# Three stacks of shifted copies, GpSimd's norm sums over six tiles, and the mean read from its PSUM bank in a convolution layer

## The chip, the cores and the metric

The kernel runs on one core of a Trainium2 chip. The metric is the device time of one execution in microseconds (us), the median of several runs. The program is a decoder trunk of two residual layers over 512 positions of 1024 channels, in float32, with nearly all of its products made of three passes over split high and low parts.

## The reference, cut to what matters

Only the second (odd) layer's mixer changes. It is a Conformer convolution module:

```python
def causal_dwconv(x, w, b):                      # depthwise: one filter of width 31 per channel
    y = lax.conv_general_dilated(x, w[:, None, :], (1,), [(k_width - 1, 0)], ..., feature_group_count=ch)
    return y + b

def layer_norm(x, g, b):                         # over the 1024 channels of each position
    mu = jnp.mean(x, axis=-1, keepdims=True)
    xc = x - mu
    return xc * lax.rsqrt(jnp.mean(xc * xc, axis=-1, keepdims=True) + EPS) * g + b

def conformer_conv(h, w_pw1, dw_w, dw_b, ln_g, ln_b, w_pw2):
    a, g = jnp.split(h @ w_pw1, 2, axis=-1)
    u = a * jax.nn.sigmoid(g)
    u = causal_dwconv(u, dw_w, dw_b)
    u = jax.nn.silu(layer_norm(u, ln_g, ln_b))
    return u @ w_pw2
```

## The kernel before

Channels lie on the 128 partitions, positions along the free axis, so that the layer's 1024 channels are eight tiles of 128x512. For each tile i of 0 to 7 the function `conv(i)` adds these tasks to a plan:

- two products with `w_pw1` (`gemm`: load the raw weights, high part on ScalarE, low part on VectorE, 24 matmuls each), scaled, put through the sigmoid and multiplied to `u` (`gated`);
- the 31 taps of the filter, shared out over the engines. The first `4*FOURS[i]` taps run on TensorE, four taps to a group: `spill` writes `u` to DRAM (`d`, two buffers), four `fetch` transfers bring it back shifted by 0 to 3 positions into a `stack` tile (four channel groups of 32, each with four shifted copies), and each task `four(m)` is four small matmuls of `stack` with diagonal weights `dg`. I call the run of these for tile i "the fours of tile i"; ahead of them two matmuls `mean(0)`, `mean(1)` (line 737) put the negative mean of the first tile into the bank as a pivot. The next `ON_G[i]` taps go through ScalarE (`tap_s`) and GpSimd (`tap_g`, line 771), and the rest through VectorE (`tap_v`, line 786) on a bank of their own where the tile is in `APART`;
- two additions (`total`, line 801) that join the parts: first `y2`, then the tile `v[:, i]`, and ScalarE's square of it (line 805).

LayerNorm needs the sum over all channels of `v` and of its square. For tiles below `ON_PE` = 4 GpSimd adds them into `sv` and `sq` (lines 821, 823); each of the tiles 4 to 7, and then `sv` and `sq`, is given to TensorE, which sums over partitions with the constant matrix `ones_m` (line 859) into two banks, `mu` and `m2`. The order there is tile 4, tile 5, the GpSimd sums, tile 6, tile 7, mean and square each.

The order of all this is not the loop's. `Plan.issue` is a small list scheduler that runs when the program is built: each task has an engine, a cost, a key (smaller goes first), tasks it follows, and slots (buffers) that it takes and gives back. It picks, among the tasks that could start within 0.15 of the earliest, the one with the smallest key, and so fixes the order of every engine's queue and of SyncE's transfers. `four` tasks have the key i - 2, the `w_pw1` products i + 0.4j - 6.2, and the sums 4.9 for the first three steps and 5.1 for the last two. There are two stacks: tile i uses `stack[i % 2]`, and its fetches wait for the fours of tile i - 2.

After the plan, VectorE reads the two banks through a 32x32 transposition (`fold`, line 177), works out the variance on 16 columns, spreads the mean again over a whole tile `mus` (`unfold`, line 181), and then goes through the eight tiles: subtract the mean (line 883), multiply by the reciprocal deviation (line 887), Silu twice on ScalarE (lines 888, 889), low part (line 892). The products with `w_pw2` (lines 934 to 938, then 159 to 161) follow. Their weights are loaded and split (lines 139, 144) outside the plan, at places that the tile framework chooses in the queues.

Of the kernel before, what the change touches and what calls it, by code (L numbers as in the profile page):

```python
# [10 lines left out]
F32 = mybir.dt.float32  # L11
F32R = mybir.dt.float32r
AF = mybir.ActivationFunctionType
ALU = mybir.AluOpType
AX = mybir.AxisListType

P = 128
T = 512
D = 1024
KT = D // P  # L20
# [7 lines left out]
CW = 31  # L28
# [68 lines left out]
def hybrid_trunk(ctx: ExitStack, tc: tile.TileContext, x, prm, w_qk, w_v, w_f, w_u, w_pool,  # L97
                 w_out, w_pw1, w_dw, w_pw2, w_up, w_down, out):
    nc = tc.nc
    V, S, G, PE = nc.vector, nc.scalar, nc.gpsimd, nc.tensor  # L100
# [79 lines left out]
    def unfold(dst, src):  # L180
        V.transpose(out=dst.rearrange("p (a b) -> p a b", b=32), in_=src.to_broadcast([P, TC, 32]))
# [7 lines left out]
    class Normed:  # L189
# [10 lines left out]
        def add(self, k):  # L200
            split(res["x"][:, k], self.h[:, k], self.l[:, k], col(self.g, self.goff + k))
            if k == 0:
                S.activation(out=self.s, in_=res["x"][:, k], func=AF.Square)
            else:
                sq = self.tmp.tile([P, T], F32, tag="tt", name="sq")
                S.activation(out=sq, in_=res["x"][:, k], func=AF.Square)
                V.tensor_tensor(out=self.s, in0=self.s, in1=sq, op=ALU.add)
# [400 lines left out]
    FOURS = (0, 2, 1, 5, 3, 4, 5, 5)  # L608
    ON_G = (14, 11, 10, 9, 8, 5, 3, 2)
    APART = (0, 1, 2, 4, 5, 6, 7)  # L610
    ON_PE = 4

    def odd_layer(nrm, next_norm):
        with tc.tile_pool(name="cnv", bufs=1) as cv, tc.tile_pool(name="cnv2", bufs=2) as c2, \
# [2 lines left out]
                tc.tile_pool(name="cnvd", bufs=2, space=bass.MemoryType.DRAM) as dr:  # L617
            v = cv.tile([P, KT, T], F32, name="v")
            ones_t = cv.tile([P, P], F32R, name="ones_t")
            w4 = cv.tile([P, KT * 32], F32, name="w4")  # L620
            nc.sync.dma_start(out=w4, in_=w_dw)
            eye = cv.tile([P, 2, 32], F32, name="eye")[:, 0:1]
            fourth = [slice(32 * q, 32 * q + 32) for q in range(4)]
            for q in fourth:
                V.tensor_copy(out=eye[q, 0], in_=ident[q, q])
            stack = [cv.tile([P, 4, CW + T], F32, name=f"stack{i}") for i in range(2)]
            for st in stack:
                G.memset(st[:, :, 0:CW], 0.0)
            sv = cv.tile([P, T], F32, name="sv")
            sq = cv.tile([P, T], F32, name="sqs")  # L630
            mus = cv.tile([P, T], F32, name="mus")
            rs = cv.tile([P, T], F32, name="rs")
            zh = cv.tile([P, KT, T], F32R, name="zh")

            dg = cv.tile([P, sum(FOURS), 4, 32], F32, tag="zl", name="dg")
            for i in range(KT):
                m0, m1 = sum(FOURS[:i]), sum(FOURS[:i + 1])
                if m0 < m1:
                    n = 4 * FOURS[i]
                    wi = w4[:, 32 * i:32 * i + n].rearrange("p (m o) -> p m o", o=1)  # L640
                    G.tensor_tensor(out=dg[:, m0:m1].rearrange("p m g c -> p (m g) c"),
                                    in0=eye.to_broadcast([P, n, 32]),
                                    in1=wi.to_broadcast([P, n, 32]), op=ALU.mult)
# [2 lines left out]
            V.tensor_copy(out=ones_t, in_=rs[:, 0:P])  # L646


            v0, v0h, v0l = mus, zh[:, KT - 2], zh[:, KT - 1]

            plan = Plan({"pe": 0.0, "v": -4.0, "s": -4.0, "g": -4.0, "sp": -12.0},
                        {"raw": 3, "wh": 3, "wl": 3, "ps": 3, "s": 4, "o": 1, "a": 2, "tt": 2,
                         "u": 4, "d": 2, "stack0": 1, "stack1": 1, "y2": 2, "tap": 6})
            add = plan.add
            r_known = add(None, 0.0, 0.0, None, lag=5.0)
            squares, gemms = {}, []
# [1 line left out]
            def conv(i, pivot, sums):  # L658
# [63 lines left out]
                u = add("v", 0.7, key, gated, t0, t1, z, lag=0.05, give=[tag0, "tt"])  # L722
# [4 lines left out]
                    nc.sync.dma_start(out=mine["d"], in_=mine["u"][:, CW - 3:])  # L727

                def fetch(n):
                    nc.sync.dma_start(out=stack[i % 2][fourth[n], :, CW:],  # L730
                                      in_=mine["d"][:, 3 - n:3 - n + T].rearrange(
                                          "(g c) t -> c g t", c=32))

                def mean(n):
                    if n == 0:
                        mine["c"] = bank("s")
                    PE.matmul(mine["c"], lhsT=ones_t, rhs=(v0h, v0l)[n], start=(n == 0), stop=False)

                def four(m):
                    for g in range(4):  # L740
                        PE.matmul(mine["c"][fourth[g]], lhsT=dg[:, sum(FOURS[:i]) + m, g],  # L741
                                  rhs=stack[i % 2][:, g, CW - 4 * m:CW - 4 * m + T],
                                  start=False, stop=(m == FOURS[i] - 1))

                used, parts = [], []
                if i > 0:
                    st = f"stack{i % 2}"
                    t = add("sp", 0.5, -9.0, spill, u, lag=2.2, take=["d"])
                    t = add(None, 0.0, 0.0, None, t, take=[st])
                    used = [add("sp", 0.45, -9.0, lambda n=n: fetch(n), t, lag=4.0)  # L750
                            for n in range(4)]
                    add(None, 0.0, 0.0, None, *used, give=["d"])
                    t = add("pe", 0.23, i - 2.0, lambda: mean(0), pivot[0], take=["s"])
                    t = add("pe", 0.23, i - 2.0, lambda: mean(1), pivot[1], t)
                    for m in range(FOURS[i]):
                        t = add("pe", 0.94, i - 2.0, lambda m=m: four(m), t, *used,
                                give=[st] * (m == FOURS[i] - 1))
                    parts.append(t)
# [11 lines left out]
                def tap_g(s):  # L770
                    G.tensor_tensor(out=mine["y2"], in0=mine["y2"], in1=mine[s], op=ALU.add)  # L771

                g = b = add("s", 0.8, i + 2.8, begin_g, u, take=["y2"])
                for s in range(s0 + 1, s1):
                    t = add("s", 0.71, i + 2.8, lambda s=s: tap_s(s), b, take=["tap"])
                    g = add("g", 1.5, i + 2.8, lambda s=s: tap_g(s), g, t, lag=0.1, give=["tap"])
# [23 lines left out]
                def total(out, acc, y2):  # L800
                    V.tensor_tensor(out=out, in0=mine[acc], in1=y2, op=ALU.add)
# [5 lines left out]
                if i > 0:  # L807
                    key = i + 2.4
                    if i in APART:
                        g = add("v", 0.7, key, lambda: total(mine["y2"], "e", mine["y2"]), g, t,  # L810
                                give=["s"])
# [5 lines left out]
                    q = add("s", 0.63, key, square, t, take=["a"])  # L817
                    if i >= ON_PE:
                        sums[2].append((t, q))
                    else:  # L820
                        sums[0] = add("g", 1.28, i + 5.0, lambda: G.tensor_tensor(
                            out=sv, in0=sv, in1=y, op=ALU.add), t, sums[0])
                        sums[1] = add("g", 1.28, i + 5.0, lambda: G.tensor_tensor(
                            out=sq, in0=sq, in1=squares[i], op=ALU.add), q, sums[1], give=["a"])
# [24 lines left out]
            pivot, sums = None, None  # L849
            for i in range(KT):  # L850
                pivot, sums = conv(i, pivot, sums)
# [4 lines left out]
            def summed(name, tag, what, first, last):  # L856
                if first:
                    ms[name] = bank(tag)
                PE.matmul(ms[name], lhsT=ones_m, rhs=what(), start=first, stop=last)  # L859

            steps = [(*sums[2][i - ON_PE], lambda i=i: v[:, i], lambda i=i: squares[i])
                     for i in range(ON_PE, KT)]
            steps.insert(2, (sums[0], sums[1], lambda: sv, lambda: sq))
            for n, (*done, a, b) in enumerate(steps):
                for j, (name, tag, what) in enumerate((("mu", "o", a), ("m2", "ps", b))):
                    first, last = n == 0, n == len(steps) - 1
                    ms[name, "t"] = add(
                        "pe", 0.87, 4.9 if n < 3 else 5.1,
                        lambda name=name, tag=tag, what=what, first=first, last=last: summed(
                            name, tag, what, first, last),  # L870
                        done[j], *((gemms[-1],) if first else (ms[name, "t"],)),
                        take=[tag] if first else [],
                        give=["a"] if j == 1 and done[j] is not sums[1] and not last else [])
# [5 lines left out]
            mu, m2 = ms["mu"], ms["m2"]  # L879
            zl = cv.tile([P, KT, T], F32R, tag="zl", name="zl")  # L880

            def less_mean(k):
                V.tensor_tensor(out=v[:, k], in0=v[:, k], in1=mus, op=ALU.subtract)

            def parts_of(k):
                y, g, b = v[:, k], col("ln_g", k), col("ln_b", k)
# [8 lines left out]
            with tc.manual_schedule(engines={ENGINES["v"]}):  # L895
                mu16 = fold(mu, c2)
                var = cv.tile([P, TC, 1], F32, name="var")
                V.tensor_tensor(out=var, in0=mu16, in1=mu16, op=ALU.mult)
                unfold(mus, mu16)
                m216 = fold(m2, c2)  # L900
                V.tensor_tensor(out=var, in0=m216, in1=var, op=ALU.subtract)
                V.tensor_scalar(out=var, in0=var, scalar1=0.0, scalar2=None, op0=ALU.max)
                less_mean(0)
                r16 = inv_sqrt(var, c2)
                unfold(rs, r16)
                parts_of(0)
                for k in range(1, KT):
                    less_mean(k)
                    parts_of(k)
                    if k > 1:  # L910
                        low_part(k - 2)
                low_part(KT - 2)
                low_part(KT - 1)
# [166 lines left out]
```

## Time and profile before

| what | value |
|---|---|
| time, median of 3 runs | 1114.05 us (1112.44 to 1114.14) |
| the profiled execution's own time | 1112.13 us |
| its span, first to last instruction | 1110.4 us |
| TensorE's matmuls busy | 1088.5 us, 98% of the span |
| VectorE busy | 739.0 us, 67% |
| ScalarE busy | 512.2 us, 46% |
| GpSimd busy | 141.0 us, 13% |
| granted TensorE clock, mean | 0.998 of full |

Busy times are sums of the instructions' own times. The convolution layer takes some 180 us of the span, from about 570 to about 750 us; GpSimd works almost only there. In the rows below, DVE is VectorE, ACT ScalarE, POOL GpSimd, PE TensorE, SPq the queue of SyncE that issues transfers, and L801 is line 801 of the kernel. "bank" is any PSUM bank. A float32 matmul is shown as two passes, so that the 20 matmuls of five fours stand as x40, and one sum of line 859 as x2.

### The profile page before, as it was taken

The numbers are of one execution on the slowest core, as the hardware profiler recorded it, in microseconds if no ns is written. First come the engines' busy times: TensorE is split into PE (matmuls) and PEld (weight loads), VectorE is DVE, ScalarE is ACT, GpSimd is POOL, SyncE is SP. The second block draws the span as 40 slices with busy tenths as digits, with TensorE's granted clock in tenths as the row PEclk, the third lists the DMA queues.
The fourth block names the chain that finished last, engine by engine and source line by source line (L and its number), as shares of the span: only waits on it lengthen the run. The fifth ranks groups of instructions, "written<-read, shape, count | busy, mean of one in ns | idle before, by whom it ended". The sixth has DMA issues, their size and how long they took to land.

```text
span 1110.4 us, 12890 instructions
## 1 busy us (share of the span) xinstructions
PE 1088.5 (98%) x4950; PEld 878.9 (79%) x4950; DVE 739.0 (67%) x1046; ACT 512.2 (46%) x717; POOL 141.0 (13%) x124
## 2 busy tenths in 40 slices
PE   9999989999999999999999998999999999999998
PEld 7777777888888888888878763788888888888886
DVE  6888986677777777433359997777777777762221
ACT  6666754444444444322238563654444444431220
POOL 0133340000000000000038994000000000000000
PEclk9999999999999999999999999999999999999999
DMA  6311025233333322333235647032233323224340
GB/s 216 104 56 39 25 79 171 95 95 95 98 101 102 97 96 90 86 104 103 93 100 147 172 110 189 9 126 94 97 100 103 99 95 95 95 86 123 105 124 19
DMA packets 37406, 111.97 MB, mean 101 GB/s; under 512 B 4192, under 2 KB 4832, under 8 KB 37344
## 3 DMA queue, kind: packets, MB, share of 16 engines
q1 hardware_dynamic: 37344, 111.14, 32.7%
q8 instruction: 39, 0.64, 0.2%
q14 instruction: 23, 0.19, 0.1%
HBM read 107.18 MB, written 3.94 MB: 100 GB/s over the span
## 4 chain that ended last, share of the span: by engine, by line
PE 88%; DVE 6%; ACT 2%; DMA 1%; issue 1%; POOL 1%; SPq 0%; ACTq 0%; POOLq 0%; DVEq 0%
PE bank L160 28%; PE bank L161 28%; PE bank L159 28%; PE bank L741 1%; POOL us L422 1%; PE bank L859 1%; DMA stack<-d 1%; DVE wl L144 1%; PE bank L934 1%; PE bank L935 0%; DMA raw<-in_w_qk 0%; ACT wh L139 0%; PE bank L540 0%; DVE fold L177 0%; PE bank L938 0%
## 5 line engine op out<-in xcount | busy, mean ns | idle before, releaser
L159 PE MATMUL bank<-xh,wh 128*128 128x512 f32 x936 | 369.1, 395 | 1.3 <-ACT wh L257 1.3
L160 PE MATMUL bank<-xl,wh 128*128 128x512 f32 x936 | 365.5, 391 | 0.0
L161 PE MATMUL bank<-xh,wl 128*128 128x512 f32 x936 | 365.4, 390 | 0.0
L139 ACT ACTIVATE wh<-raw 128x1024 fp32r<-128x1024 f32 (+2 forms) x186 | 190.2, 1025 | 266.7 <-PE bank L160 229.3
L144 DVE TENSOR_TENSOR wl<-raw,wh 128x1024 fp32r<-128x1024 f32 (+1 forms) x176 | 213.9, 1217 | 141.3 <-ACT wh L139 139.4
L159 PEld LDWEIGHTS bank<-xh,wh 128*128 128x128 f32 x936 | 176.2, 188 | 41.4 <-issue 2.3
L161 PEld LDWEIGHTS bank<-xh,wl 128*128 128x128 f32 x936 | 176.0, 188 | 37.3 <-issue 0.7
L160 PEld LDWEIGHTS bank<-xl,wh 128*128 128x128 f32 x936 | 176.2, 188 | 37.0 <-issue 1.4
L159 PE MATMUL bank<-ah,wh 128*128 128x512 f32 x352 | 136.9, 389 | 0.0
L160 PE MATMUL bank<-al,wh 128*128 128x512 f32 x352 | 136.9, 389 | 0.0
L161 PE MATMUL bank<-ah,wl 128*128 128x512 f32 x352 | 136.9, 389 | 0.0
L971 DVE SCALAR_TENSOR_TENSOR y<-u,pt,y 128x511 f32<-128x511 f32 (+1 forms) x176 | 131.6, 748 | 7.8 <-ACT y L968 4.7
L966 DVE TENSOR_TENSOR u<-bank,rstd 128x512 f32<-128x512 f32 x88 | 60.5, 688 | 79.1 <-PE bank L161 79.1
L771 POOL TENSOR_TENSOR y<-y,tap 128x512 f32<-128x512 f32 x54 | 80.2, 1487 | 12.8 <-ACT tap L768 9.6
L166 ACT ACTIVATE ah<-y 128x512 fp32r<-128x512 f32 x44 | 27.8, 632 | 115.0 <-DVE y L976 115.0
L159 PEld LDWEIGHTS bank<-ah,wh 128*128 128x128 f32 x352 | 66.1, 188 | 13.8
L161 PEld LDWEIGHTS bank<-ah,wl 128*128 128x128 f32 x352 | 66.1, 188 | 13.7
L160 PEld LDWEIGHTS bank<-al,wh 128*128 128x128 f32 x352 | 66.1, 188 | 13.6
L968 ACT ACTIVATE y<-u,pt 128x512 f32<-128x512 f32 x88 | 71.3, 810 | 5.0 <-DVE u L966 3.9
L975 ACT ACTIVATE y<-y 128x512 f32<-128x512 f32 x44 | 27.8, 633 | 82.9 <-DVE y L971 82.8
L219 DVE TENSOR_TENSOR xr<-bank,xr 128x512 f32<-128x512 f32 x32 | 22.0, 690 | 60.5 <-PE bank L161 60.5
L786 DVE SCALAR_TENSOR_TENSOR bank<-u,pt,bank 128x512 f32<-128x512 f32 x79 | 56.4, 749 | 1.5 <-ACT bank L782 0.8
(197 smaller groups left out, 1061.3 us busy)
## 6 DMA issues: line engine op xcount, KB each, us to landing
raw<-in_w_up SPq DMA_DIRECT2D x88, 512.0 KB, 3.4
raw<-in_w_down SPq DMA_DIRECT2D x32, 512.0 KB, 3.5
raw<-in_w_pw SPq DMA_DIRECT2D x24, 512.0 KB, 3.8
stack<-d SPq DMA_DIRECT2D x28, 256.0 KB, 4.9
raw<-in_w_down SPq DMA_DIRECT2D x16, 384.0 KB, 3.2
xr<-in_x SPq DMA_DIRECT2D x16, 256.0 KB, 5.6
raw<-in_w_out SPq DMA_DIRECT2D x8, 512.0 KB, 3.4
raw<-in_w_qk SPq DMA_DIRECT2D x6, 512.0 KB, 3.5
```

Source lines behind the costliest of these rows:

```text
L139: S.activation(out=wh, in_=raw, func=AF.Copy)
L144: on.tensor_tensor(out=wl, in0=raw, in1=wh.bitcast(F32), op=ALU.subtract)
L159: PE.matmul(acc, lhsT=ah, rhs=bh, start=(first and i == 0), stop=False)
L160: PE.matmul(acc, lhsT=ah, rhs=bl, start=False, stop=False)
L161: PE.matmul(acc, lhsT=al, rhs=bh, start=False, stop=(last and i == n - 1))
L166: S.activation(out=h, in_=src, func=AF.Copy)
L771: G.tensor_tensor(out=mine["y2"], in0=mine["y2"], in1=mine[s], op=ALU.add)
L786: V.scalar_tensor_tensor(out=acc, in0=shifted(s), scalar=wcol(s), in1=acc, op0=ALU.mult, op1=ALU.add)
L966: V.tensor_tensor(out=u, in0=acc, in1=nrm.r, op=ALU.mult)
L968: S.activation(out=y, in_=u, func=AF.Identity, scale=col("cv_w", 3 * ct + 2), bias=col("cv_b", ct))
L971: V.scalar_tensor_tensor(out=y[:, s:], in0=u[:, 0:T - s], scalar=col("cv_w", 3 * ct + 2 - s), in1=y[:, s:], op0=ALU.mult, op1=ALU.add)
L975: S.activation(out=ys[0], in_=ys[0], func=AF.Silu)
```

## The change

- A third stack: tile i uses `stack[i % 3]`, so that its fetches wait for the fours of tile i - 3.
- `ON_PE` is 6: GpSimd adds the tiles 0 to 5, and TensorE sums only tile 6, the GpSimd sums, and tile 7, in this order. The first two of these steps have the key 4.9.
- VectorE subtracts the mean from `mu`, the PSUM bank itself; the tile `mus` and the `unfold` into it are gone.
- Memory: `dg`, `sv` and `w4` become parts of one tile `room` in the place that `zl` takes later, and the first tile's intermediate `v0` lies in `v[:, 7]` instead of `mus`.

```diff
-    ON_PE = 4
+    ON_PE = 6
...
-            w4 = cv.tile([P, KT * 32], F32, name="w4")
+            room = cv.tile([P, KT * T], F32, tag="zl", name="room")
+            DG = sum(FOURS) * P
+            dg = room[:, 0:DG].rearrange("p (m g c) -> p m g c", g=4, c=32)
+            sv = room[:, DG:DG + T]
+            w4 = room[:, DG + T:DG + T + KT * 32]
...
-            stack = [cv.tile([P, 4, CW + T], F32, name=f"stack{i}") for i in range(2)]
+            stack = [cv.tile([P, 4, CW + T], F32, name=f"stack{i}") for i in range(3)]
...
-            sv = cv.tile([P, T], F32, name="sv")
-            mus = cv.tile([P, T], F32, name="mus")
-            dg = cv.tile([P, sum(FOURS), 4, 32], F32, tag="zl", name="dg")
...
-            v0, v0h, v0l = mus, zh[:, KT - 2], zh[:, KT - 1]
+            v0, v0h, v0l = v[:, KT - 1], zh[:, KT - 2], zh[:, KT - 1]
...
-                         "u": 4, "d": 2, "stack0": 1, "stack1": 1, "y2": 2, "tap": 6})
+                         "u": 4, "d": 2, "stack0": 1, "stack1": 1, "stack2": 1, "y2": 2, "tap": 6})
...
-                    nc.sync.dma_start(out=stack[i % 2][fourth[n], :, CW:],
+                    nc.sync.dma_start(out=stack[i % 3][fourth[n], :, CW:],
...
-                                  rhs=stack[i % 2][:, g, CW - 4 * m:CW - 4 * m + T],
+                                  rhs=stack[i % 3][:, g, CW - 4 * m:CW - 4 * m + T],
...
-                    st = f"stack{i % 2}"
+                    st = f"stack{i % 3}"
...
-            steps.insert(2, (sums[0], sums[1], lambda: sv, lambda: sq))
+            steps.insert(-1, (sums[0], sums[1], lambda: sv, lambda: sq))
...
-                        "pe", 0.87, 4.9 if n < 3 else 5.1,
+                        "pe", 0.87, 4.9 if n < len(steps) - 1 else 5.1,
...
-                V.tensor_tensor(out=v[:, k], in0=v[:, k], in1=mus, op=ALU.subtract)
+                V.tensor_tensor(out=v[:, k], in0=v[:, k], in1=mu, op=ALU.subtract)
...
-                unfold(mus, mu16)
```

## Rows read from the trace of the kernel before

**Rows 1.** A window of 10 us: busy of PE, PEld, DVE, ACT, POOL; clock; DMA share, GB/s.

```profile
670.00:680.00 10.00, 6.88 (x50) 2.24 (x50) 9.46 (x15) 5.74 (x9) 9.48 (x8) 1.00 0.80 179
```

**Rows 2.** The chain that ended last, 671 to 698 us: start, length, what.

```profile
672.54 6.61 DMA stack<-d
...
679.28 4.50 PE bank L741 x40
683.77 4.49 PE bank L859 x10
...
688.73 4.43 PE bank L741 x40
693.16 2.79 PE bank L859 x6
...
695.97 0.73 DVE fold L177
...
696.91 0.62 DVE mus L181
```

**Rows 3.** Timeline of PE: start, length, instructions, idle time before.

```profile
656.99 4.50 PE L741 MATMUL bank<-stack,dg 128*32 128x512 f32 x40
...
667.55 2.78 PE L741 MATMUL bank<-stack,dg 128*32 128x512 f32 x24
672.61 0.74 PE L737 MATMUL bank<-zh,ones_t 128*128 128x512 f32 x2 [2.28 <-DVE v L801]
673.28 3.64 PE L741 MATMUL bank<-stack,dg 128*32 128x512 f32 x32
676.85 1.13 PE L859 MATMUL bank<-v,ones_m 128*128 128x512 f32 x2
```

**Rows 4.** Timeline of SP, the queue that issues transfers.

```profile
653.45 0.34 SPq L727 DMA_DIRECT2D d<-u  x1
...
670.71 0.34 SPq L727 DMA_DIRECT2D d<-u  x1
...
676.98 1.83 SPq L730 DMA_DIRECT2D stack<-d  x4
```

**Rows 5.** Transfers issued in 671 to 673, then 676 to 679 us: KB, median us to landing.

```profile
d<-u SPq DMA_DIRECT2D x1, 257.5 KB, 3.0
...
stack<-d SPq DMA_DIRECT2D x4, 256.0 KB, 4.7
```

**Rows 6.** Timeline of DVE in the same stretch and behind it.

```profile
666.40 2.26 DVE L144 TENSOR_TENSOR wl<-raw,wh 128x1024 fp32r<-128x1024 f32 x1
...
676.99 0.69 DVE L801 TENSOR_TENSOR v<-bank,y 128x512 f32<-128x512 f32 x1 [0.54 <-PE bank L741]
677.60 4.04 DVE L786 SCALAR_TENSOR_TENSOR bank<-u,pt,bank 128x512 f32<-128x512 f32 x6
681.55 0.68 DVE L801 TENSOR_TENSOR y<-bank,y 128x512 f32<-128x512 f32 x1
...
686.88 0.69 DVE L801 TENSOR_TENSOR y<-bank,y 128x512 f32<-128x512 f32 x1
687.49 2.35 DVE L144 TENSOR_TENSOR wl<-raw,wh 128x1024 fp32r<-128x1024 f32 x2
...
700.70 0.68 DVE L883 TENSOR_TENSOR v<-v,mus 128x512 f32<-128x512 f32 x1
```

**Rows 7.** Timeline of ACT, while the eight tiles are normed.

```profile
702.87 1.51 ACT L889 ACTIVATE v<-v,pt 128x512 f32<-128x512 f32 x2
```

**Rows 8.** Timeline of POOL, its last instruction.

```profile
679.22 1.29 POOL L771 TENSOR_TENSOR y<-y,tap 128x512 f32<-128x512 f32 x1 [0.28 <-ACT tap L768]
```

**Rows 9.** Groups by line, 660 to 705 us: busy, mean ns, idle before.

```profile
L801 DVE TENSOR_TENSOR v<-bank,y 128x512 f32<-128x512 f32 x5 | 3.5, 690 | 5.6 <-PE bank L741 5.5
...
L883 DVE TENSOR_TENSOR v<-v,mus 128x512 f32<-128x512 f32 x4 | 2.7, 684 | 0.0
L821 POOL TENSOR_TENSOR sv<-sv,v 128x512 f32<-128x512 f32 x2 | 2.6, 1305 | 0.0
```

## The prediction

> **What bounds the kernel now.** I read the page first: TensorE's matmuls are busy for 98% of the span, so the time moves only where TensorE waits, or where it does work that can be left out. The windows of 10 us over the convolution layer then show where it waits: up to 670 us it is full, and from 670 to 680 us it is busy for 6.88 of 10 us, while VectorE (9.46) and GpSimd (9.48) are nearly full [rows 1]. So until 670 us this layer is held by TensorE with VectorE and GpSimd close behind, and at its end something else decides.
>
> The chain of waits names it. A transfer into a stack, issued at 672.54 us, takes 6.61 us to land, and the fours of tile 6 start on it at 679.28. Then TensorE runs without a break: fours of tile 6, five sums of line 859 (x10, 4.49 us, so 0.90 each), the pivot (0.47, what is left between 683.77 + 4.49 and 688.73), fours of tile 7 (4.43), three more sums until the mean is complete. At 695.97 VectorE begins the statistics [rows 2].
>
> The timeline of TensorE shows what lay ahead. The fours of tile 4 end at 670.33; the pivot of tile 5 waits 2.28 us for a bank that an addition on VectorE frees; the fours of tile 5 end at 676.9. Then come one sum (tile 4) and the wait for the stack [rows 3]. VectorE is not late there: it waits 0.54 us for TensorE at 676.99, ends its tile-6 work at 682.2 and its last `y2` addition at 687.5 [rows 6], and the statistics still start 8 us later. GpSimd ends at 680.5 [rows 8]. I call the time from the start of the fours of tile 6 to the first `fold` the tail: 695.97 - 679.28 = 16.69 us.
>
> **The third stack.** The fetches of tile 6 waited for the fours of tile 4 (670.33), although its `u` had been spilled at 653.45 [rows 3, 4]. With three stacks they wait for the fours of tile 3, over at 661.5 [rows 3]. Even with the 6.61 us of the slowest landing, and four issues, they are there by about 670, before TensorE needs them. The fours of tile 6 then follow those of tile 5 directly. The tile-4 sum goes to GpSimd, so the pivot starts at 676.85 and the fours at 677.32: **-1.96 us**. The other bound: the pivot's bank might be the one that VectorE frees at 676.99 + 0.69 = 677.68 [rows 6], which gives 678.15 and -1.13. I take the first, since an earlier addition should free another of the four.
>
> Tile 7 is what could be late next. Its spill is issued at 670.71 [rows 4] and lands in 3.0 us [rows 5]. The fetches, which waited for the fours of tile 5 until 676.98 [rows 4], can go at about 673.7 and the last at 675.1. With a median landing of 4.7 us [rows 5] they are there at 679.8, with 6.61 [rows 2] at 681.7. The fours of tile 7 can start at 677.32 + 4.49 + 0.47 = 682.28. So it is hidden, by 0.6 us at the worst. On SyncE's queue the `w_pw2` weights stand behind these fetches and move earlier by the same 3 us.
>
> The fetches of tiles 3 to 5 also come earlier, but the order on TensorE there is set by the keys, and it is full: nothing.
>
> **The sums.** Two tiles' sums, four of line 859, leave TensorE. One stood before the tail and is counted above. Inside the tail the work is now: fours 4.49, pivot 0.47, fours 4.43, the four sums of tile 6 and of GpSimd's results 3.60, and the tile-7 mean 0.93 (2.79 / 3) [rows 2]: 13.92. That holds only if the addition that completes tile 7 hides behind sums. The keys speak against it: 4.9 is below the 5.0 of tile 7's fours, so the four sums slip in among these and nothing is left to cover the addition of 0.69 us [rows 9] and its hand-over, some 0.8 together. I take 14.72, hence **-1.97 us**, with -2.77 as the other end.
>
> GpSimd gets four additions, each 1.305 us [rows 9], 5.2 in all, and would end at 680.51 + 5.2 = 685.7 [rows 8]. It is full up to there, so the cover is the lead it has over TensorE: after fours of tile 6 (681.81), pivot, one four (0.89) and the two sums of tile 6, TensorE asks for `sv` at about 685.0 and for `sq` at 685.9. Just hidden; each further us of GpSimd's would show. Behind that sum in TensorE's queue stand the rest of tile 7's fours. The sums of tile 4 may push tile 7's one GpSimd tap to about 683, ahead of VectorE's `y2` addition at 686.88 [rows 6].
>
> VectorE has tile 6 complete when? Its addition to `y2` ends at 682.2 [rows 6], so tile 6 is ready at 682.9, and TensorE asks for it at 683.2. Hidden too.
>
> **The mean from its bank.** The `unfold` of 0.62 us on the chain goes [rows 2]; the other `fold` then starts 0.62 earlier, about when the last square sum is done: **-0.62 us**, with nothing as the other end. The subtraction with an operand in PSUM is not in the trace, but additions with one PSUM operand take 690 ns against 684 for today's subtraction [rows 9]: nothing. [...]
>
> **Memory.** `dg`, `sv` and `w4` in one tile cost nothing if waits are kept by region. They seem to be: VectorE subtracts in the second slice of `v` at 700.70 [rows 6] although ScalarE's write to the first, earlier in the program, runs only at 702.87 [rows 7].
>
> **Sum.** -1.96 - 1.97 - 0.62 = -4.55, say -4.6 us. Behind 701 us TensorE is full again and the rest moves along. The profiled execution took 1112.13 us (span 1110.4, 1.7 around it), so it would become 1107.5; it lies 1.9 below the median of the runs, 1114.05, from which I forecast **1109.4 us**. Own bounds: -1.13 - 1.97 - 0 = -3.1 and -1.96 - 2.77 - 0.62 = -5.4, so 1108.6 to 1111.0.
>
> **Rivals.**
>
> *More than that.* One low part of `w_pw2` weights (line 144) sits at 666.40 on VectorE and takes 2.26 us, against 1.2 each for the two at 687.49 [rows 6]. It delays the addition that frees the bank at 672.61. The tile framework sets its place anew; if it goes behind tile 7, up to 2.26 us more are gained: 1107.2 to 1108.1 with a half to all of it.
>
> *No change: VectorE becomes late.* The weights' low parts may instead come in front of tile 6's additions, since their loads move 3 us earlier. At 2.26 us each while GpSimd runs, two make tile 6 ready at 682.9 + 4.5 = 687.4, and TensorE, whose queue has the tile-6 sum behind the first four of tile 7, stands from 683.2 to 687.4. Of this 4.2 nothing is covered: -0.4 us, 1113.7. [...]
>
> *The stack does not do it.* If `room` is tracked as a whole, the fours (which read `dg`) wait for GpSimd's writes to `sv` that precede them in the program. Those of tile 6 would wait for GpSimd's tile-4 sum, which comes when it is free at 678.94 (679.22 less 0.28 of idle time [rows 8]) and ends at 680.2: the start is 1.0 us later than now instead of 1.96 earlier, and the sum is +1.0 - 1.97 - 0.62 = -1.6: 1112.5. The slices of `v` speak against it.
>
> *Slower.* A low part placed on VectorE ahead of the six taps at 677.60 would also stand waiting for weights, which now are split only at 687.49 to 689.84 [rows 6]. Taps (4.04), two additions for tile 6, three taps and two additions for tile 7 are some 8.7 us; from 689.84 tile 7 is ready at 698.5 and the mean at 699.5, against 695.97: +3.5 - 0.62 = +2.9, 1116.9. It decides once VectorE comes back to its taps after about 687.0 (695.97 + 0.62 - 0.93 - 8.7). Today it has weights' parts at places that wait little, which speaks against it.
>
> **How the numbers follow.** Forecast 0.58, more 0.14, late VectorE 0.13, whole tile 0.08, slower 0.07. About 0.2%, 2.2 us, is what a measurement of this kernel can tell from no change. Faster by more: 0.58 + 0.14 + half of the whole-tile case, 0.76; within 0.2%: 0.13 + 0.04, 0.17; slower: 0.07. The range goes from 1106.0 (the larger gain, less 1 us of the runs' own spread) to 1113.7, the case of the late VectorE; beyond it lie the slower case and the tails of the others, under 0.2.
>
> **What would show it.** Right: fetches of tile 6 issued near 661.5 us and of tile 7 near 674; no wait of line 741 for a transfer; fours of tile 6 near 677.3; six sums of line 859; GpSimd at work to about 685.7; `fold` of the mean near 692, the second `fold` straight after it. Wrong: a wait of TensorE for the tile-6 addition or for GpSimd at line 859, a low part of 2 us between 677 and 683 on VectorE, a fours task waiting for GpSimd.

## The result, and the profile after

The changed kernel takes **1123.59 us** (median of 4 runs, 1120.31 to 1124.08) against 1113.47 (4 runs, 1112.44 to 1114.14): ratio 1.0088, 95% interval 1.0071 to 1.0105. It is slower by some 10 us, where 1109.4 was forecast. The profiled execution has a span of 1122.3 us against 1110.4, so 11.9 more. Of all executions timed below, one of run 8 took 5059.93 us; it stands apart from the rest and is left out of that run's median.

The page gives little: the busy times are nearly those of before, and the mean granted clock of TensorE is 0.992 of full instead of 0.998. The chain of waits says more (start, length, what):

```profile
679.71 7.95 DMA d<-u
...
689.02 5.58 DMA stack<-d
...
694.74 1.94 PE bank L743 x8
696.68 2.00 PE bank L861 x2
698.68 1.87 PE bank L743 x8
700.55 1.08 PE bank L861 x2
701.63 1.00 PE bank L743 x8
```

Before, the transfer on the chain was a stack of tile 6, landed at 679.15 [rows 2]. Now it is tile 7's spill, issued 9 us later than before (679.71 against 670.71 [rows 4]), which takes 7.95 us instead of 3.0 [rows 5], and tile 7's stack behind it. The matmuls after it come in two speeds: eight of line 743 take 1.94 us, and a little later 1.00.

The timeline of TensorE for the same stretch (the brackets are the idle time before, and what ended it):

```profile
679.83 1.03 PE L739 MATMUL bank<-zh,ones_t 128*128 128x512 f32 x2 [4.79 <-DVE v L803]
680.79 4.95 PE L743 MATMUL bank<-stack,room 128*32 128x512 f32 x32
...
686.34 4.50 PE L743 MATMUL bank<-stack,room 128*32 128x512 f32 x40
...
694.74 1.94 PE L743 MATMUL bank<-stack,room 128*32 128x512 f32 x8 [3.24 <-DMA stack<-d]
```

The fours of tile 6 start at 686.34, not at the forecast 677.32: the pivot of tile 5 waits 4.79 us for VectorE's addition (2.28 before [rows 3]), and that of tile 4 had waited 2.92 us for one (none before). Then the fours of tile 7 wait 3.24 us for a stack. Who is late? First the queue of SyncE, after and then before:

```profile
632.53 0.33 SPq L729 DMA_DIRECT2D d<-u  x1
636.86 7.67 SPq L134 DMA_DIRECT2D raw<-in_w_pw  x2
644.63 1.83 SPq L732 DMA_DIRECT2D stack<-d  x4
...
650.48 5.35 SPq L134 DMA_DIRECT2D raw<-in_w_pw  x2
655.94 1.82 SPq L732 DMA_DIRECT2D stack<-d  x4
661.84 0.34 SPq L729 DMA_DIRECT2D d<-u  x1
662.23 15.43 SPq L134 DMA_DIRECT2D raw<-in_w_pw  x2
677.77 1.82 SPq L732 DMA_DIRECT2D stack<-d  x4
679.71 0.36 SPq L729 DMA_DIRECT2D d<-u  x1
687.72 1.73 SPq L732 DMA_DIRECT2D stack<-d  x4
```

```profile
653.89 0.40 SPq L134 DMA_DIRECT2D raw<-in_w_pw  x1
661.56 1.76 SPq L730 DMA_DIRECT2D stack<-d  x4
...
671.15 1.81 SPq L730 DMA_DIRECT2D stack<-d  x4
...
678.91 11.32 SPq L134 DMA_DIRECT2D raw<-in_w_pw  x5
```

Before, five of the six `w_pw2` loads stand behind the last fetch, where nothing of this layer is behind them. Now all six stand between the spills and fetches of tiles 4 to 7. Line 134 loads into a buffer that a low part on VectorE (line 144) must give back, as the waits of SyncE's queue from 590 to 700 us say (in all, times, longest; after, then before):

```profile
SPq L134 <- DVE wl L144: 56.4, 10, 14.5
```

```profile
SPq L134 <- DVE wl L144: 28.8, 7, 5.8
```

Here the queue keeps its order: the last two loads occupy it from 662.23 to 677.66, and tile 6's fetches behind them go at 677.77, 6.6 us later than before (671.15), although the fours of tile 3, which had used their stack, were over at 663.04 and tile 6's spill, issued at 661.84, had landed after 4.0 us. So tile 7's spill goes right behind these fetches and takes 7.95 us, and tile 7's own fetches wait for it until 687.72. Of the 9 us by which the spill is late, the queue accounts for less than 2: VectorE has tile 7's `u` ready only at 677.86 (line 715).

Second, VectorE and ScalarE:

```profile
653.62 1.80 DVE L144 TENSOR_TENSOR wl<-raw,wh 128x1024 fp32r<-128x1024 f32 x1 [2.50 <-ACT wh L139]
...
659.72 1.46 DVE L144 TENSOR_TENSOR wl<-raw,wh 128x1024 fp32r<-128x1024 f32 x1 [0.39 <-ACT wh L139]
...
675.67 1.59 DVE L144 TENSOR_TENSOR wl<-raw,wh 128x1024 fp32r<-128x1024 f32 x1 [0.36 <-ACT wh L139]
...
679.10 0.68 DVE L803 TENSOR_TENSOR v<-bank,y 128x512 f32<-128x512 f32 x1
...
708.71 0.72 DVE L177 STREAM_TRANSPOSE fold<-bank 128x512 f32<-128x512 f32 x1 [1.22 <-PE bank L861]
...
709.56 0.72 DVE L177 STREAM_TRANSPOSE fold<-bank 128x512 f32<-128x512 f32 x1
```

```profile
652.53 1.06 ACT L139 ACTIVATE wh<-raw 128x1024 fp32r<-128x1024 f32 x1 [3.58 <-PE bank L160]
```

Three low parts of `w_pw2` stand in VectorE's queue ahead of tile 4's last addition, where one did [rows 6]. The first waits 2.50 us for its high part, which waits 3.58 us on ScalarE for TensorE's products (line 160), whose weights lie in the buffer it is to fill. Waits (2.50 + 0.39 + 0.36 = 3.25) and the longer work (1.80 + 1.46 + 1.59, less the 2.26 of before, = 2.59) are 5.8 us. Tile 4's addition comes 7.2 us later (679.10, 671.87 before). The difference of some 1.5 is there already when the layer begins; the table below puts it down to the single execution and not to the change.

### The profile page after: what moved, and what is told of

Same layout as the page of the kernel before. It is cut to its first block, busy times and chain, and to the rows that moved or that the text cites. A ratio compares the mean times of both kernels' runs of the same rounds, so it can differ in the third digit from the quotient of the medians.

```text
span 1122.3 us, 12878 instructions
## 1 busy us (share of the span) xinstructions
PE 1091.2 (97%) x4942; PEld 877.1 (78%) x4942; DVE 740.6 (66%) x1045; ACT 511.6 (46%) x717; POOL 147.0 (13%) x129
## 4 chain that ended last, share of the span: by engine, by line
PE 87%; DVE 6%; ACT 2%; DMA 2%; POOL 1%; issue 1%; SPq 0%; ACTq 0%; POOLq 0%; DVEq 0%
PE bank L159 28%; PE bank L160 27%; PE bank L161 27%; PE bank L743 1%; DVE bank L788 1%; DMA d<-u 1%; POOL us L422 1%; PE bank L861 1%; ACT wh L139 1%; DVE wl L144 1%; PE bank L540 1%; DMA stack<-d 0%; PE bank L935 0%; PE bank L936 0%; POOL y L773 0%
## 5 line engine op out<-in xcount | busy, mean ns | idle before, releaser
L144 DVE TENSOR_TENSOR wl<-raw,wh 128x1024 fp32r<-128x1024 f32 (+1 forms) x176 | 216.2, 1230 | 144.2 <-ACT wh L139 142.2
```

The lines of the kernel that those rows point to most:

```text
L144: on.tensor_tensor(out=wl, in0=raw, in1=wh.bitcast(F32), op=ALU.subtract)
```

## The experiments

All lost time shows up ahead of the second `fold`. The table sets the moments of each profiled execution side by side, in us (start of the fours of tile 6; the two `fold` instructions of line 177; the last three columns are differences from before). What the second `fold` moves, the span moves, within 0.4. "Ahead" is the part of it that is there already at the norm's sum at the start of the layer (line 211, at 573.02 us before). It lies between -0.6 and +1.7 us, and it is +1.5 in the changed kernel but +0.2 in run 8, which has the same order of loads; so I take it for a difference between executions. "Fold moved" less "ahead" is what happens in the layer, and it lies within 1 us of what the ratios of the timed runs say. Each ratio is against the kernel before timed beside that run: medians of 1112.15 us for runs 1 to 4, 1112.97 for 5 to 8, 1112.82 for 9 and 10.

| kernel | fours of tile 6 | first fold | tail | second fold | fold moved | ahead | span moved |
|---|---|---|---|---|---|---|---|
| before | 679.28 | 695.97 | 16.69 | 697.45 | | | |
| after | 686.34 | 708.71 | 22.37 | 709.56 | +12.1 | +1.5 | +11.9 |
| 1 two stacks | 678.95 | 695.29 | 16.34 | 696.15 | -1.3 | -0.5 | -1.2 |
| 2 stacks alone | 687.74 | 704.44 | 16.70 | 705.29 | +7.8 | +1.7 | +7.6 |
| 3 pinned | 675.58 | 691.25 | 15.67 | 692.11 | -5.3 | -0.6 | -5.3 |
| 4 before, early loads | 681.16 | 696.99 | 15.83 | 698.48 | +1.0 | +1.4 | +1.0 |
| 5 parts early, loads late | 686.75 | 703.10 | 16.35 | 703.96 | +6.5 | +1.3 | +6.1 |
| 6 pinned, sums of before | 676.70 | 692.54 | 15.84 | 693.40 | -4.1 | -0.2 | -4.1 |
| 7 sums last, low on GpSimd | 676.23 | 690.35 | 14.12 | 691.25 | -6.2 | +0.1 | -6.1 |
| 8 TensorE kept busy | 685.51 | 705.20 | 19.69 | 706.06 | +8.6 | +0.2 | +8.4 |
| 9 sums last | 675.65 | 689.77 | 14.12 | 690.63 | -6.8 | -0.5 | -6.8 |
| 10 low on GpSimd | 677.12 | 693.46 | 16.34 | 696.31 | -1.1 | +0.9 | -1.1 |

Theory A was that the places of the `w_pw2` loads and parts make the loss. Its rivals, B and C, put it on what two stacks would keep as well: the sums on GpSimd and among tile 7's fours, the shared tile `room` and the mean read from its bank.

**1. The change with two stacks.**

```diff
-            stack = [cv.tile([P, 4, CW + T], F32, name=f"stack{i}") for i in range(3)]
+            stack = [cv.tile([P, 4, CW + T], F32, name=f"stack{i}") for i in range(2)]
...
-                    st = f"stack{i % 3}"
+                    st = f"stack{i % 2}"
```

> The changed kernel with two stacks again (the GpSimd sums over six tiles, the mean from its bank and the shared memory stay). Theory A: the third stack alone let the tile framework move the w_pw2 weights' loads, high and low parts between the convolution's transfers, and these stall SyncE's queue and VectorE. Then this kernel has the loads where the kernel before has them, its fours of tile 6 still wait for their stack, and it is 1 to 3 us faster than before (the tail 1 to 2 us shorter, the unfold 0.6). Theory B: GpSimd, full up to 680 us, pays for 5.2 us more of sums, and everything behind it is late. Then it stays 5 to 10 us slower than before. Theory C: the subtraction from PSUM or the shared tile costs the time; then also some 5 to 10 us slower.

1111.31 us (11 runs) against 1112.15, ratio 0.9993 (0.9984 to 1.0002). The loss is gone, and the loads are at before's places (one at 654.51, five from 678.92), so B and C fall. But the 1 to 3 us that A expected are missed, and the sums' forecast gain is not there either: the tail is 16.34, only 0.35 less than before. TensorE's timeline shows why:

```profile
678.95 4.50 PE L742 MATMUL bank<-stack,room 128*32 128x512 f32 x40 [2.10 <-DMA stack<-d]
...
684.04 1.06 PE L742 MATMUL bank<-stack,room 128*32 128x512 f32 x8
685.03 1.13 PE L860 MATMUL bank<-v,ones_m 128*128 128x512 f32 x2
686.09 1.06 PE L742 MATMUL bank<-stack,room 128*32 128x512 f32 x8
```

Fours (matrices of 128x32) and sums (128x128) alternate, and a pair takes 2.05 us, 684.04 to 686.09. In blocks of their own they are 0.89 (4.43 / 5) and 0.90 [rows 2], 1.79 together. Each pair thus takes 0.26 us more where the two shapes alternate, four pairs 1.0, of the 1.6 us that the tail is longer than forecast. The prediction had not weighed it.

**2. Three stacks, with the sums of before.** `ON_PE` is 4 again and the order of the sums that of before; `room` and the mean from its bank stay.

```diff
-    ON_PE = 6
+    ON_PE = 4
...
-            steps.insert(-1, (sums[0], sums[1], lambda: sv, lambda: sq))
+            steps.insert(2, (sums[0], sums[1], lambda: sv, lambda: sq))
```

> The changed kernel with the sums as before (GpSimd adds four tiles, TensorE sums four and the order of before): the third stack, the shared memory and the mean from its bank stay. Theory A: the loads move as in the changed kernel, so it is 8 to 12 us slower than before. Theory B: the sums were the cost, so it is 2 to 3 us faster than before (the wait for the stack gone, the unfold gone). Theory C: slower by 5 to 10 us.

1119.24 us (4 runs), ratio 1.0054 (1.004 to 1.0068). The third stack brings a loss without the moved sums: a block of 15.44 us for two loads from 662.41, and the same 4.79 us of the pivot of tile 5. It is 6.0 us and not the 8 to 12 that A expected. The tail is 16.70, since before's order has sums to run while tile 7's stack is still on its way. With the loads in these places the moved sums thus cost 3.8 us more (9.8 less 6.0; tails of 22.37 and 16.70): they no longer stand where TensorE has to wait.

**3. The change, with `w_pw2` held at before's places.** The first three loads, high and low parts become tasks of the plan, behind the tasks that they followed before; the other loads stay behind the last fetch.

```diff
                 pivot, sums = conv(i, pivot, sums)
+            weights(0, 0, -20.0, ("spill", 6), ("sq", 3), ("y2", 4))
+            weights(2, 0, 20.0, ("fetch", 7), ("sq", 6), ("y2", 7))
+            weights(4, 0, 20.0, ("fetch", 7), ("sq", 6), ("y2", 7))
```

(A `weights` task set has a load, a high and a low part, each behind the named task.)

> The whole change, with the first three w_pw2 loads and their high and low parts made tasks of the plan, at the places that they have in the kernel before: the first load behind the spill of tile 6, its low part behind the y2 addition of tile 4, the other two behind the last fetch, their low parts behind the y2 addition of tile 7. Theory A: the time of the prediction, 3 to 5 us faster than before, the fours of tile 6 directly behind those of tile 5, no wait of VectorE for a high part before 680 us. Theories B and C: it stays 8 us or more slower than before, since sums, memory and subtraction are all those of the changed kernel.

1107.33 us (5 runs), ratio **0.9953** (0.994 to 0.9967): some 5.2 us faster than before and 15 faster than the change as it stood, with nothing altered but these places and that the plan knows of them. SyncE's queue and TensorE:

```profile
661.01 1.75 SPq L734 DMA_DIRECT2D stack<-d  x4
...
672.99 1.73 SPq L734 DMA_DIRECT2D stack<-d  x4
```

```profile
674.92 0.73 PE L741 MATMUL bank<-zh,ones_t 128*128 128x512 f32 x2 [0.90 <-DVE y L807]
675.58 4.50 PE L745 MATMUL bank<-stack,room 128*32 128x512 f32 x40
...
690.09 1.13 PE L897 MATMUL bank<-v,ones_m 128*128 128x512 f32 x2 [0.81 <-DVE v L807]
```

Tile 6's fetches go at 661.01 and tile 7's at 672.99, as forecast, and no fours wait for a transfer. The fours of tile 6 are not quite directly behind those of tile 5: their pivot waits 0.90 us for an addition on VectorE.

**4. The kernel before, with its loads early.** The counterpart: all six loads, and three pairs of parts, as tasks of the plan, two loads behind the spill of tile 4, two behind that of tile 5, two behind that of tile 6.

```diff
+            weights(0, 0, -20.0, ("spill", 4), ("spill", 4), ("spill", 4))
+            weights(2, 0, -20.0, ("spill", 4), ("spill", 4), ("spill", 4))
+            weights(4, 0, -20.0, ("spill", 5), ("spill", 5), ("spill", 5))
+            weights(0, 4, -20.0, ("spill", 5))
...
```

> The kernel before, with nothing of the change, but with six w_pw2 loads as tasks of the plan, early: the first two behind the spill of tile 4, two behind that of tile 5, two behind that of tile 6, and the high and low parts of the first three as soon as the plan has them. Theory A: slower than before by 5 to 12 us, VectorE's and SyncE's waits as in the changed kernel, tile 4 complete 3 to 6 us later than before. Theories B and C: within 1 us of before.

1112.94 us (10 runs), ratio 1.0001 (0.9992 to 1.001). This missed: early loads as such cost nothing. The plan knows them here, with a cost and with the buffers that they take, and orders the other tasks around them: none of the three low parts waits for its high part, and SyncE is never held longer than 6.62 us by two loads. So theory A had to be narrowed: the loss comes from loads and parts set into the queues, between tasks whose order was fixed without them. Run 5 is the test of this.

**5. The parts as in the change, loads four to six behind the last fetch.**

```diff
+            for n in (0, 2, 4):
+                raw_late(n)
```

(`raw_late` makes a load a task behind the last fetch of tile 7; the first three loads and their parts keep the places that they had in the change, as tasks of cost 0, so that the plan makes no room for them.)

> The whole change, with the first three w_pw2 loads, their high and low parts where the changed kernel has them, but the loads four to six behind the last fetch on SyncE's queue instead of in front of the spill and fetches of the tiles 6 and 7. It keeps what ScalarE and VectorE lose by the early parts, and takes away what SyncE's queue loses. Theory: the parts alone make tile 4 complete 5 to 6 us late, and the fours of tile 6 start as late as in the changed kernel; but tile 7's stack is there in time, TensorE has no gap of 3 us ahead of its fours, and its clock stays up there. So 6 to 7 us less than the changed kernel: 3 to 5 us slower than before. Rival 1, SyncE's queue is the whole loss: 4 to 5 us faster than before. Rival 2, VectorE's lateness is the whole loss: 9 to 10 us slower, as the changed kernel.

1117.68 us (4 runs), ratio 1.0041 (1.0025 to 1.0058): 4.6 us slower than before, within the 3 to 5 expected. SyncE fetches tile 6 at 664.51, tile 7's spill is no longer issued right behind these fetches, and tile 7's fetches go 2.4 us behind the spill instead of 8.0:

```profile
678.03 0.34 SPq L733 DMA_DIRECT2D d<-u  x1
680.42 3.15 SPq L736 DMA_DIRECT2D stack<-d  x4
```

Yet VectorE is as late as in the change:

```profile
653.38 2.11 DVE L144 TENSOR_TENSOR wl<-raw,wh 128x1024 fp32r<-128x1024 f32 x1 [3.56 <-ACT wh L139]
...
679.20 0.68 DVE L812 TENSOR_TENSOR v<-bank,y 128x512 f32<-128x512 f32 x1
```

Against the pinned kernel, the first three loads with their parts cost 0.0088 of 1113 us, some 9.8 us, and loads four to six another 0.0047, some 5.2, each known to within some 2.5 us by its intervals. Together with -5.2 from the change itself this is the +9.8 of the result. In the table the first cost lies ahead of the fours of tile 6 (686.75 against 675.58) and the second in the tail (22.37 against 16.35): 3.24 us of waiting for tile 7's stack, and the slow matmuls behind it (run 8).

**6. Pinned, with the sums of before.** The kernel of run 3 and the diff of run 2:

```diff
-    ON_PE = 6
+    ON_PE = 4
...
-                        "pe", 0.87, 4.9 if n < len(steps) - 1 else 5.1,
+                        "pe", 0.87, 4.9 if n < 3 else 5.1,
```

> The pinned kernel of the whole change with the sums as before: GpSimd adds four tiles, TensorE sums tiles 4 and 5 too, in the order of before. What it loses against the pinned kernel is what the moved sums bring once the loads are in place. By the prediction's tail (1.97 us) and the tile-4 sum that comes back between the fours of tiles 5 and 6 (0.9) it is 2 to 3 us slower than the pinned kernel, so 2 to 3 us faster than before. Rival: between tile 7's fours each sum and each four takes some 0.1 us longer, as in the kernel with two stacks, which eats most of the gain; then it is within 1.5 us of the pinned kernel, 3.5 to 4.5 us faster than before.

1109.01 us (9 runs), ratio 0.9967 (0.9956 to 0.9979). Third stack and mean from its bank alone thus give some 3.7 us, not 2 to 3 but what the rival said, and moving two tiles' sums to GpSimd adds only about 1.5. The intervals of the two kernels overlap, so that the 1.5 is not clear of noise; in the profiled executions it is 0.9 (-4.8 against -3.9, what was ahead of the layer taken off).

**7 and 9. Pinned, and all sums behind the fours of tile 7.** Run 9 alters the key alone; run 7 also moves the three low parts to GpSimd.

```diff
-                        "pe", 0.87, 4.9 if n < len(steps) - 1 else 5.1,
+                        "pe", 0.87, 5.1,
```

> The pinned kernel with all six sums behind the fours of tile 7 (key 5.1 for every step), and the low parts of the first three w_pw2 weights on GpSimd, behind its last sums. The sums then cover the addition that completes tile 7 (0.8 us) and do not take turns with the fours (some 1 us): 1 to 2 us faster than the pinned kernel, 6 to 7 us faster than before. Rival: GpSimd's three low parts, 2.6 us or more each from about 686 us, are late for the first w_pw2 products near 694 us, and it is no faster than the pinned kernel or slower.

> The change with the weights' loads and parts held at the places of before (as in the pinned run), and all sums given the key 5.1, so that they run behind the fours of tile 7 in one block; the low parts stay on VectorE. If the order of sums and fours is what the version with sums last gained (alternating costs some 0.6 us of switching and leaves the 0.8 us of tile 7's addition bare), this run has that version's time, 6.1 to 6.4 us below the kernel before, and a tail near 14.1 us; VectorE's two low parts in front of tile 7's last addition are over by about 687.1 and hidden under sums until 689.3. If the gain came from taking the low parts off VectorE, it stays at the pinned run's 4.8 to 5.2 us below.

Run 7: 1106.61 us (6 runs), ratio 0.9945 (0.993 to 0.996). Run 9: **1105.85 us** (5 runs), ratio 0.9946 (0.9934 to 0.9959), the version to keep, with a tail of 14.12:

```profile
680.74 4.50 PE L745 MATMUL bank<-stack,room 128*32 128x512 f32 x40
685.17 1.12 PE L897 MATMUL bank<-v,ones_m 128*128 128x512 f32 x2
```

```profile
685.31 0.69 DVE L807 TENSOR_TENSOR v<-bank,y 128x512 f32<-128x512 f32 x1 [0.41 <-PE bank L745]
...
689.77 0.72 DVE L177 STREAM_TRANSPOSE fold<-bank 128x512 f32<-128x512 f32 x1 [0.82 <-PE bank L897]
```

The fours run without a change of shape, and VectorE's addition for tile 7 (685.31) lies behind four sums instead of bare before the last ones. In the timed runs the pinned kernel (0.994 to 0.9967) and this one (0.9934 to 0.9959) overlap; the step is seen only in the tail of the two profiled executions, 15.67 to 14.12.

**8. The change, with TensorE kept busy during its wait.** Fifteen small products of no use, into an idle bank, between pivot and fours of tile 7.

```diff
+                def busy():
+                    idle = bank("ps")
+                    for _ in range(15):
+                        PE.matmul(idle[:, 0:P], lhsT=ones_m, rhs=ones_m, start=True, stop=True)
```

> The changed kernel, with 15 small matmuls of constants into an unused bank between the pivot and the fours of tile 7, where TensorE stands 3 us for the stack. They take away no wait. If the half clock in the fours of tile 7 comes from that standing, the granted clock stays near 1 from 692 to 704 us and the kernel is 2.5 to 3.5 us faster than the changed kernel, 6 to 8 us slower than before. If the clock has another cause, it falls as in the changed kernel, and the time is the same as its, about 10 us slower than before.

1121.59 us (3 runs), ratio 1.0076 (1.0058 to 1.0095). Windows of 4 us (busy of PE, PEld, DVE, ACT, POOL, then the granted clock, DMA share, GB/s) of the change, then of this run:

```profile
676.00:680.00 4.00, 0.17 (x1) 0.17 (x2) 4.00 (x6) 1.59 (x4) 3.84 (x4) 1.00 0.43 125
680.00:684.00 4.00, 4.00 (x22) 1.04 (x26) 3.66 (x6) 2.43 (x4) 3.92 (x4) 0.57 1.03 235
...
692.00:696.00 4.00, 1.26 (x8) 0.23 (x8) 2.72 (x4) 0.59 (x1) 0.00 (x0) 0.72 0.41 77
696.00:700.00 4.00, 4.00 (x14) 0.70 (x10) 0.00 (x0) 0.00 (x0) 0.00 (x0) 0.50 0.00 0
```

```profile
692.00:696.00 4.00, 4.00 (x29) 2.28 (x27) 1.67 (x3) 0.00 (x0) 0.00 (x0) 1.00 0.00 0
696.00:700.00 4.00, 4.00 (x21) 0.91 (x20) 0.00 (x0) 0.00 (x0) 0.00 (x0) 1.00 0.02 4
```

In the change TensorE's granted clock is 0.50 from 696 to 700 us, behind a window in which it worked 1.26 of 4 us. In run 8 the clock stays at 1.00. From the start of tile 7's fours to the first `fold` the change takes 708.71 - 694.74 = 13.97 us, run 8 705.20 - 693.95 = 11.25: the clock cost 2.7 us in this execution. In the timed runs the two kernels are 1.3 us apart, less than the 2.5 to 3.5 expected, and their intervals overlap, so the clock's share in the median is not shown.

**10. Pinned, low parts on GpSimd, sums at the change's keys.**

```diff
-            weights(0, 0, -20.0, ("spill", 6), ("sq", 3), ("y2", 4))
+            weights(0, 0, 20.0, ("fetch", 7), ("sq", 6), ("sq", 6), "g")
...
```

> The change with the loads held at the places of before and the three low parts on GpSimd, behind its sums, with the sums at the change's own keys, among the fours of tile 7. If the order of sums and fours is what the version with sums last gained, this run stays near the pinned run, 4.8 to 5.2 us below the kernel before, with a tail near 15.7 us. If the low parts were the gain, it is 6.1 to 6.4 us below.

1111.51 us (11 runs), ratio 0.9989 (0.998 to 0.9998), which misses both values. The tail is 16.34, since here every four alternates with a sum, as in run 1. The rest is a small instruction of VectorE between the two folds that ran while GpSimd made a low part:

```profile
694.21 2.17 DVE L936 TENSOR_TENSOR var<-fold 128x16 f32<-128x16 f32 x1
```

```profile
693.99 2.35 POOL L144 TENSOR_TENSOR wl<-raw,wh 128x1024 fp32r<-128x1024 f32 x1 [4.45 <-ACT wh L139]
```

In run 9 this multiplication of 128x16 takes 0.19 us. Here it ends with GpSimd's instruction, at 696.4. It makes no case for the low parts as run 7's gain; run 9, which has run 7's tail with the low parts on VectorE, puts that gain on the order of the sums.

## Why the prediction was wrong, point by point

**The step that failed** is the one on SyncE's queue, that the `w_pw2` weights stand behind the fetches "and move earlier by the same 3 us", and with it the judgement under "Slower" that weights' parts stand "at places that wait little, which speaks against it". Where they stood before was no evidence for where they would stand after. With a third stack all six loads come between the spills and fetches, and the first three low parts ahead of tile 4's last addition. Runs 2, 3 and 5 show it: 9.8 us for the first three loads with their parts, 5.2 for loads four to six. Why a third stack makes the tile framework choose these places was not settled; the runs show only that it does so with three stacks and not with two.

**"Slower" was the nearest rival**: a low part that waits in front of VectorE's taps, at the wrong place and a third of the price. It was put at 677 us ahead of six taps of tile 6 (+2.9), and three were at 653 to 676 us; the first waited for a high part whose buffer TensorE's products still held, and not for late weights. That a queue of transfers would be held up as well was in no rival, and neither was the fall of TensorE's clock. My chances for it, 0.07, and for a VectorE that is late at tile 6, 0.13, rested on the places of before.

**The third stack**, -1.96: with the places held, the fours of tile 6 start 3.70 us earlier (run 3). About 0.6 of this is there already ahead of the layer. The rest beyond 1.96 comes from the pivot of tile 5, which no longer waits 2.28 us for VectorE [rows 3]; I had left that wait in place. In exchange the pivot of tile 6 waits 0.90 us for an addition on VectorE, much as my other bound for this term had it. Why the one wait went is not shown. The rival of `room` tracked as a whole did not occur: no fours waited for GpSimd.

**The sums**, -1.97: mis-sized. Measured by the tail it is -1.02 in run 3 and -0.35 in run 1. What was left out is the change between fours and sums, 0.26 us a pair; it is most of what is missing in run 1. The tail of 14.72 that I named is reached, and passed, only when the sums run in one block (14.12, runs 7 and 9), and then the bare addition of 0.8 us is covered too, the "other end" of that term.

**The mean from its bank**, -0.62: right. The second `fold` follows the first after 0.85 us (709.56 - 708.71) instead of 1.48, so 0.63. The subtraction with its operand in PSUM takes 0.68 us in all runs, as the one without did [rows 9].

**GpSimd**: in run 3 its additions take 1.28 us, priced at 1.305 [rows 9]. It is at work until 684.4 us, against 685.7 forecast, and TensorE does not wait for it there.

So the sum of the three parts, -4.55, stands at -4.8 in the profiled execution of run 3 (-5.3 less the 0.6 from ahead of the layer) and -5.2 in its ratio: near the forecast for the kernel that I had described, which was not the kernel that the diff made. That it is so near is in part luck: the third stack gave some 1.2 us more than its term and the sums some 1.0 less. One figure of the rivals was also added up wrongly: half of the 2.26 us in "More than that" gives 1108.3, not 1108.1.

## What to carry to other kernels

An order written out by a scheduler holds only for the tasks it knows. Where another layer places loads and their conversions into the same queues, any change of buffers can move them: list what stands in each queue after the change before costing it, and give such work to the scheduler as tasks, or pin it. And when matmuls of two shapes share TensorE, try each shape in a block, with the block that depends on nothing late placed over the wait: here an alternating pair took 0.26 us more than in blocks (run 1), and one block of sums brought the tail from 15.67 to 14.12 us (runs 3 and 9).

## What the hardware showed that was not expected

- A spill of 257.5 KB that lands in 3.0 us [rows 5] took 7.95 in the changed kernel, issued directly behind the four fetches of another tile.
- TensorE's granted clock fell to 0.50 behind a stretch with 1.26 of 4 us busy, and eight passes of line 743 took 1.94 us there instead of 1.00. At 680 to 684 us it was 0.57, behind 0.17 of 4 us busy, and the fours of tile 5 took 4.95 us instead of 3.64 [rows 3].
- A 128x16 multiplication on VectorE took 2.17 us instead of 0.19 beside a 128x1024 subtraction on GpSimd (run 10, once).
- Alternating fours (128x32) and sums (128x128) cost 0.26 us for each pair (run 1).
